# Both feed-forward blocks in two phases, with gated activations stored to DRAM and seven-product sums formed in PSUM

## The chip, the cores and the metric

The kernel runs on one core of a Trainium2 chip. The metric is device time in microseconds for one execution. TensorE (PE) does the matmuls, VectorE (DVE), ScalarE (ACT) and GpSimd (POOL) the elementwise work, SyncE (SP) issues the DMAs. The time before is the median of three runs.

## What is computed

The program is a two-layer encoder trunk over 1024 tokens of width 1024, in float32: in each layer an attention block and a SwiGLU feed-forward block (FFN), both with a modulated RMS norm ahead and a gated residual add behind, and a last RMS norm.

```python
D_FF = 2816
def swiglu(h, w_in, w_out):
    gate, up = jnp.split(h @ w_in, 2, axis=-1)
    return (jax.nn.silu(gate) * up) @ w_out

for i in range(DEPTH):                       # DEPTH = 2
    ...
    h = rmsnorm(x, norm2_g[i]) * (1.0 + scale2) + shift2
    x = x + gate2 * swiglu(h, f_w_in[i], f_w_out[i])
return rmsnorm(x, final_g)
```

## The kernel before

A float32 operand is split into a high part (ACT cast, L95) and a low part (VectorE subtract, L96), and a product is three matmuls: high by high, high by low, low by high (`mm3`, L98 to L107). Activations lie transposed, 128 features by 512 tokens; the tokens are two halves, c = 0 and 1. Weights come in raw blocks of 256 KB (five slots, `RAW`), are combined on POOL where a combination is wanted (L833), and split into one of four pairs of tiles (`RP`).

The FFN (`ffn`, L843) has 22 steps f, one for 128 gate and 128 up features. For f = 2 to 20 the first matmul (1024 by 256 of weights, by 1024 by 1024) is done by `fast(f)`: seven products of half-size blocks in place of eight. Each is 4 x 3 = 12 matmuls of 512 columns, and its operands are combinations of blocks: those of the activations are made once by `norm_parts` (L754) at the start of the FFN, those of the weights by `w_operands` for each f. f = 0, 1 and 21 are done by `plain(f, c)`, four block products for each half of the tokens. The seven products of `fast` rotate over seven half-banks of PSUM (`prod`: two tiles S of two banks each, two T, one A). The sums of products are formed by VectorE adds in SBUF (L902, L918) with a few ACT copies (L926, L928, L941), then Silu and the product gate by up.

After each two f, `out(p)` does the second matmul for their 256 features: four w_out blocks, 96 matmuls, into banks T, T, M in turn (`ffn_out`, L1033), each result added to the residual by VectorE (L1036, `gate2 * ps + x`). These matmuls are placed by priority between the products of the next f. The program's order on each engine is set by a scheduler at build time, from the order of the code and from priority offsets (`WAHEAD`: weight work 60 places earlier). A PSUM tile is waited for as a whole: a user of a tile that is written again waits for the last reader of the tile.

In layer 0 the modulation of layer 1 is computed within the FFN: `ada_half` gives small steps, two per f, each with a raw load, an ACT activation (L147) and a POOL add (L149). In layer 1 the last `out` is split by token half, c = 1 in two quarters; after each the norm's squares are summed (L176, L180), the row sum is formed on PE (L184), VectorE and POOL form the factor (L198, L200), and `final` (L1018) scales and stores.

Of the kernel before, what the change touches and what calls it, by code (L numbers as in the profile page):

```python
# [30 lines left out]
DAHEAD = 0  # L31
MAHEAD = 60
# [6 lines left out]
TAILP = 0, 4  # L39
# [19 lines left out]
class Trunk:  # L59
# [38 lines left out]
    def mm3(self, ps, w, xs, n, w0=0, first=True, last=True):  # L98

        whi, wlo = w  # L100
        mm = self.nc.tensor.matmul
        for k in range(n):
            ws = slice((w0 + k) * P, (w0 + k + 1) * P)
            xh, xl = xs[k]
            mm(ps, lhsT=whi[:, ws], rhs=xh, start=first and k == 0, stop=False)  # L105
            mm(ps, lhsT=whi[:, ws], rhs=xl, start=False, stop=False)  # L106
            mm(ps, lhsT=wlo[:, ws], rhs=xh, start=False, stop=last and k == n - 1)  # L107
# [65 lines left out]
    def norm_acc(self, pool, x, d, box, eng=None, n=CH):  # L173
        nc = self.nc
        sq = self.t(pool, "ft", [P, CH])
        nc.scalar.activation(out=sq[:, :n], in_=x, func=AF.Square)  # L176
        if d == 0:
            box["sq"] = sq
        else:
            (eng or nc.gpsimd).tensor_tensor(out=box["sq"][:, :n], in0=box["sq"][:, :n], in1=sq[:, :n], op=ALU.add)  # L180
# [11 lines left out]
    def norm_rb(self, sq, n=4, ps=None):  # L192
        nc = self.nc
        if ps is None:
            ps = self.bank("A")
        self.rowsum(ps, sq, n)
        v = self.t(self.sp, "v8", [P, 4])
        self.v_ins = nc.vector.tensor_scalar(out=v[:, :n], in0=ps[:, :n], scalar1=1.0 / D, scalar2=EPS, op0=ALU.mult, op1=ALU.add)  # L198
# [552 lines left out]
    def norm_parts(self, ft, bslot, tmp, xs, rb, av, bv, c, h0, ops):  # L751

        nc = self.nc
        h1 = {}  # L754
# [12 lines left out]
        def comb(i, a, b, op, eng=None, eng2=None):  # L767
            t = self.t(ft, "ft", [P, CH])
            (eng or nc.vector).tensor_tensor(out=t, in0=a, in1=b, op=op)
            return lambda: put(i, t, eng2)  # L770

        def step0(d):
            h0[d] = h_of(d, bslot(F32))
            if d < 4:
                put(2, h0[d])
            else:
                comb(4, h0[d], h0[d - 4], ALU.subtract)()

        def step1(d):
            e, f = h_of(d, self.t(ft, "ft", [P, CH])), h_of(d + 4, tmp())  # L780
            comb(3, e, f, ALU.subtract)()
            put(5, f)
            comb(6, h0[d], e, ALU.add, nc.gpsimd, nc.gpsimd)()
            h1[d] = f

        def step2(d):
            f = h1[d]
            p1 = comb(1, h0[d], f, ALU.add, nc.gpsimd)
            p7 = comb(7, h0[d + 4], f, ALU.add)
            p1()  # L790
            p7()
# [14 lines left out]
    def w_split(self, src):  # L806
        hi, lo = self.w_pair()
        raw = self.w_tile(src)
        with self.tc.high_priority(offset=WAHEAD):
            self.split(hi, lo, raw)  # L810
        return hi, lo

    def w_operands(self, layer, f):

        raw = {}

        def blk(i, j):
            if (i, j) not in raw:
# [3 lines left out]

        comb = {1: (1, 1, 2, 2, ALU.add, False), 2: (2, 1, 2, 2, ALU.add, True), 5: (1, 1, 1, 2, ALU.add, False),
                6: (2, 1, 1, 1, ALU.subtract, False), 7: (1, 2, 2, 2, ALU.subtract, True)}

        def get(i):
            hi, lo = self.w_pair()
            if i in comb:
                a, b, c, d, op, last = comb[i]
                x, y = blk(a, b), blk(c, d)  # L830
                t = x if last else y if i == 6 else self.t(self.rw, "raw", [P, CH])
                with self.tc.high_priority(offset=WAHEAD):
                    self.nc.gpsimd.tensor_tensor(out=t, in0=x, in1=y, op=op)  # L833
                    self.split(hi, lo, t)
            else:
                x = blk(*{3: (1, 1), 4: (2, 2), 8: (1, 2), 9: (2, 1)}[i])
                with self.tc.high_priority(offset=WAHEAD):
                    self.split(hi, lo, x)
# [4 lines left out]
    def ffn(self, layer, wo, xdst):  # L843
# [3 lines left out]
        with tc.tile_pool(name="hb", bufs=22, reuse_waits="tile") as hb, \  # L847
# [33 lines left out]
            gs = [[], []]  # L881
            unit = {}
            tt = nc.vector.tensor_tensor
            f_tile = lambda: self.t(ft, "ft", [P, CH])

            flip = [0]

            def prod(i, get):

                n = flip[0] % 7  # L890
                flip[0] += 1
                if n < 4:
                    if n % 2 == 0:
                        unit["S"] = self.t(self.pss, "S")
                    ps = unit["S"][:, n % 2 * CH:(n % 2 + 1) * CH]
                else:
                    ps = self.bank("TTA"[n - 4])
                self.mm3(ps, get(i), ops[i], 4)
                return ps

            def add(t, ps):
                tt(out=t, in0=t, in1=ps, op=ALU.add)  # L902

            def plain(f, c):
# [3 lines left out]
                for h, (i, j) in enumerate((((5, 2), (8, 4)), ((2, 2), (4, 4))) if c == 0 else (((5, 5), (3, 3)), ((9, 3), (2, 5)))):  # L908
# [3 lines left out]
                g = f_tile()  # L912
                nc.scalar.activation(out=g, in_=ps[:, :CH], func=AF.Silu)
                glu(c, g, ps[:, CH:])

            def glu(c, x, y):
                hi, lo = self.t(gp, "g", [P, CH], F32R), self.t(gp, "g", [P, CH], F32R)
                tt(out=x, in0=x, in1=y, op=ALU.mult)  # L918
                self.split(hi, lo, x)
                gs[c].append((hi, lo))  # L920

            def fast(f, mid):

                get = self.w_operands(layer, f)
                gate1, up1, gate0, up0 = (f_tile() for _ in range(4))
                nc.scalar.copy(out=gate1, in_=prod(3, get))  # L926
                p = prod(1, get)
                nc.scalar.copy(out=gate0, in_=p)  # L928
                tt(out=up1, in0=gate1, in1=p, op=ALU.add)
                mid()  # L930
                p = prod(5, get)
                tt(out=gate0, in0=gate0, in1=p, op=ALU.subtract)
                add(gate1, p)
                nc.scalar.activation(out=gate1, in_=gate1, func=AF.Silu)
                add(up1, prod(6, get))
                if ada:
                    ada.pop(0)()
                add(gate0, prod(7, get))
                p = prod(2, get)
                tt(out=up1, in0=up1, in1=p, op=ALU.subtract)  # L940
                nc.scalar.copy(out=up0, in_=p)  # L941
                p = prod(4, get)
                add(gate0, p)
                add(up0, p)
                if ada:
                    ada.pop(0)()
                nc.scalar.activation(out=gate0, in_=gate0, func=AF.Silu)
                glu(1, gate1, up1)
                glu(0, gate0, up0)

            def w_out(p, h):
                return self.w_split(a["w_out"][layer, p, h])

            def out(p):
                cur = [gs[0][:], gs[1][:]]
                gs[0].clear(), gs[1].clear()

                def go():
                    for h in range(4):
                        w = w_out(p, h)  # L960
                        for d in (2 * h, 2 * h + 1):
                            for c in range(2):
                                self.ffn_out(w, cur[c], d, gate2, xs[c][d])

                return go

            for c in range(2):
                for f in range(LEAD):
                    plain(f, c)
# [7 lines left out]
            for c in range(2):  # L977
                plain(NF - 1, c)
            if layer == 0:
                self.make_a(self.avec[1][0], self.sm[:, C_N1 + 8:C_N1 + 16], self.mods[1][1])  # L980
            hn = [[None] * KT, [None] * KT]
            todo = [lambda: None] * KT if layer == 0 else []
            ws = [w_out(NF // 2 - 1, h) for h in range(4)]
            parts = [(0, 0, CH), (1, 0, CH)] if layer == 0 else [(0, 0, CH), (1, 0, CH // 2), (1, CH // 2, CH)]
            for part, (c, n0, n1) in enumerate(parts):
                box = {}
                n = n1 - n0
                xc = [x[:, n0:n1] for x in xs[c]]
                gc = [(hi[:, n0:n1], lo[:, n0:n1]) for hi, lo in gs[c]]
                cs = slice(c * CH + n0, c * CH + n1)  # L990
                if layer:
                    ps = self.t(self.pss, "S") if part else self.bank("A")
                for d in range(KT):
                    self.ffn_out(ws[d // 2], gc, d, gate2, xc[d], n)
                    if layer == 0:
# [207 lines left out]
```

## Time and profile before

| | |
|---|---|
| median of 3 runs | 2751.7 us (2749.83 to 2757.51) |
| the profiled execution | 2753.28 us, span 2751.2 us |
| granted TensorE clock, mean | 0.970 |
| PE busy | 2600.1 us, 95% |
| DVE, ACT, POOL busy | 70%, 43%, 36% |
| DMA, mean | 71 GB/s |

The span runs from the first to the last instruction of the profiled execution. Busy shares are means over the whole program; the FFN of layer 0 fills about 840 to 1480 us of it, that of layer 1 about 2070 to 2740 us. A matmul's shown length (0.39 us for 512 columns) is not its price, since matmuls are pipelined: the distance between two starts is.

### The profile page before, as it was taken

To read this page: it belongs to the slowest core of one execution; us is meant where nothing else is said; L and a number is where in the kernel's file an instruction comes from. 1 tells how busy PE (TensorE), PEld (TensorE's weight loads), DVE (VectorE), ACT (ScalarE), POOL (GpSimd) and SP (SyncE) were. 2 spreads that over 40 slices of the span, in tenths; PEclk is the share of its full clock that TensorE was granted. 3 is DMA by queue.
4 is the path that set the end of the run, shared out by engine and by line. 5 is a ranking of instruction groups with operands and counts; after the bars stand their busy time and mean duration, and the time that the engine had idled before them with its cause. 6 is when DMAs were issued, how large, how long until landed. Compare 5 with 4: busy or idle time off the path is not lost.

```text
span 2751.2 us, 34376 instructions
## 1 busy us (share of the span) xinstructions
PE 2600.1 (95%) x12888; PEld 2138.1 (78%) x12888; DVE 1913.9 (70%) x2921; ACT 1193.2 (43%) x2049; POOL 988.7 (36%) x664
## 2 busy tenths in 40 slices
PE   6799999999998999999999899999998999999997
PEld 5577777777776888888887788888877888888886
DVE  6777777777667667676666777577567666666666
ACT  5455555555443333333334565555443333332323
POOL 7634444531154223232223456433153222222222
PEclk9899999999998999999999999999999999999998
DMA  6211211112211222221214222213211111111112
GB/s 255 74 44 49 70 50 59 63 42 96 78 49 58 66 65 74 65 69 62 71 64 146 96 73 89 85 59 110 70 35 50 54 50 58 54 50 54 50 58 85
DMA packets 86582, 195.89 MB, mean 71 GB/s; under 512 B 9488, under 2 KB 11792, under 8 KB 86416
## 3 DMA queue, kind: packets, MB, share of 16 engines
q1 hardware_dynamic: 86416, 193.71, 20.7%
q8 instruction: 101, 1.65, 0.3%
q14 instruction: 65, 0.53, 0.1%
HBM read 177.94 MB, written 15.73 MB: 70 GB/s over the span
## 4 chain that ended last, share of the span: by engine, by line
PE 76%; DVE 12%; ACT 3%; POOL 3%; DMA 2%; issue 2%; SPq 0%; DVEq 0%; ACTq 0%; POOLq 0%
PE T L105 7%; PE T L106 7%; PE T L107 7%; PE S L106 6%; PE S L105 6%; PE S L107 6%; PE M L105 6%; PE M L106 5%; PE M L107 5%; PE S L548 3%; PE T L256 3%; PE A L270 2%; PE A L268 2%; PE A L269 2%; DVE mx L556 2%
## 5 line engine op out<-in xcount | busy, mean ns | idle before, releaser
L833 POOL TENSOR_TENSOR raw<-raw,raw 128x512 f32<-128x512 f32 x214 | 299.2, 1399 | 877.5 <-DMA raw<-in_w_in 552.1
L95 ACT CAST whi<-raw 128x512 fp32r<-128x512 f32 x402 | 249.0, 621 | 672.1 <-PE T L106 215.7
L96 DVE TENSOR_TENSOR wlo<-raw,whi 128x512 fp32r<-128x512 f32 x402 | 330.3, 826 | 124.8 <-ACT whi L95 124.4
L105 PE MATMUL M<-h,whi 128*128 128x512 f32 x616 | 252.6, 410 | 8.6 <-ACT tmp L470 4.2
L1036 DVE SCALAR_TENSOR_TENSOR h<-T,mod,h 128x512 f32<-128x512 f32 (+1 forms) x270 | 197.7, 733 | 70.8 <-PE T L107 69.6
L107 PE MATMUL M<-h,wlo 128*128 128x512 f32 x616 | 244.6, 397 | 1.0 <-POOL wlo L96 1.0
L105 PE MATMUL S<-h,whi 128*128 128x512 f32 x572 | 226.7, 397 | 19.5 <-DVE ft L918 19.3
L106 PE MATMUL M<-h,whi 128*128 128x512 f32 x616 | 244.9, 398 | 0.0
L95 ACT CAST pt<-T 128x512 fp32r<-128x512 f32 x256 | 145.3, 588 | 211.5 <-PE T L256 211.0
L106 PE MATMUL S<-h,whi 128*128 128x512 f32 x572 | 227.5, 398 | 5.0 <-DVE h L214 3.1
L96 DVE TENSOR_TENSOR pt<-T,pt 128x512 fp32r<-128x512 f32 x256 | 171.6, 682 | 80.7 <-ACT pt L95 80.4
L107 PE MATMUL S<-h,wlo 128*128 128x512 f32 x572 | 226.2, 396 | 0.0
L105 PE MATMUL T<-g,whi 128*128 128x512 f32 (+1 forms) x540 | 210.7, 390 | 10.2 <-DVE h L1036 8.8
L106 PE MATMUL T<-g,whi 128*128 128x512 f32 (+1 forms) x540 | 208.3, 386 | 1.4 <-DVE g L96 1.4
L107 PE MATMUL T<-g,wlo 128*128 128x512 f32 (+1 forms) x540 | 207.9, 385 | 0.0
L129 POOL TENSOR_TENSOR wraw<-wraw,cond 128x1024 f32<-128x1024 f32 x64 | 155.9, 2437 | 126.9 <-DMA wraw<-in_ada_t 119.6
L556 DVE TENSOR_REDUCE mx<-S 128x1 f32<-128x1024 f32 x128 | 150.2, 1215 | 44.3 <-PE S L548 44.2
L270 PE MATMUL A<-pt,v 128*128 128x256 f32 x512 | 155.6, 304 | 23.2 <-DVE pt L96 23.2
L559 ACT ACTIVATE e<-S,mx 128x1024 f32<-128x1024 f32 x128 | 141.4, 1111 | 71.7 <-DVE mx L558 71.7
L256 PE MATMUL T<-ident,e 128*128 128x128 f32 x1024 | 149.1, 280 | 13.3 <-DVE pt L96 10.1
L268 PE MATMUL A<-pt,v 128*128 128x256 f32 x512 | 156.3, 305 | 4.3 <-ACT pt L95 4.2
L269 PE MATMUL A<-pt,v 128*128 128x256 f32 x512 | 151.4, 296 | 0.0
(290 smaller groups left out, 6445.7 us busy)
## 6 DMA issues: line engine op xcount, KB each, us to landing
raw<-in_w_in SPq DMA_DIRECT2D x200, 256.0 KB, 2.8
wraw<-in_ada_t SPq DMA_DIRECT2D x64, 512.0 KB, 3.2
raw<-in_w_out SPq DMA_DIRECT2D x88, 256.0 KB, 2.6
wraw<-in_wqkvA SPq DMA_DIRECT2D x23, 512.0 KB, 3.2
aq<-in_ada_s SPq DMA_DIRECT2D x16, 512.0 KB, 4.9
raw<-in_ada_w SPq DMA_DIRECT2D x32, 256.0 KB, 2.6
wraw<-in_wqkvB SPq DMA_DIRECT2D x15, 512.0 KB, 3.3
o<-tmp SPq DMA_DIRECT2D x28, 256.0 KB, 2.0
```

The lines of the kernel that those rows point to most:

```text
L95: self.nc.scalar.copy(out=hi, in_=src)
L96: (eng or self.nc.vector).tensor_tensor(out=lo, in0=src, in1=hi.bitcast(F32), op=ALU.subtract)
L105: mm(ps, lhsT=whi[:, ws], rhs=xh, start=first and k == 0, stop=False)
L106: mm(ps, lhsT=whi[:, ws], rhs=xl, start=False, stop=False)
L107: mm(ps, lhsT=wlo[:, ws], rhs=xh, start=False, stop=last and k == n - 1)
L256: nc.tensor.transpose(ps[:, i * P:(i + 1) * P], w[:, k * P:(k + 1) * P], self.ident)
L268: mm(ps, lhsT=vh[:, ks], rhs=hi, start=(k == 0), stop=False)
L269: mm(ps, lhsT=vl[:, ks], rhs=hi, start=False, stop=False)
L270: mm(ps, lhsT=vh[:, ks], rhs=lo, start=False, stop=(k == KT - 1))
L556: nc.vector.tensor_reduce(out=mx, in_=ps, op=ALU.max, axis=AX.X, negate=True)
L833: self.nc.gpsimd.tensor_tensor(out=t, in0=x, in1=y, op=op)
L1036: self.nc.vector.scalar_tensor_tensor(out=x, in0=ps, scalar=gate2[:, d:d + 1], in1=x, op0=ALU.mult, op1=ALU.add)
```

## The change

The FFN is done in two phases. Phase 1 computes all gated activations: `fast` for f = 2 to 21 with another scheme of seven products, in which four of the sums are formed in PSUM (`more=True` goes on adding to a bank that holds a former product). One tile S holds x and z, a bank T holds y. ACT copies a state of x or z to SBUF before the next product is added to it. Four POOL combinations of weights per f remain of five. The gated activations and their combinations are stored to DRAM (`keep`, seven kinds for each of eleven pairs of f, 154 stores of 256 KB in all).

Phase 2 computes the second matmul as seven block products over all of k: for each of eleven k a left operand (w_out blocks, `left`), a right one (loaded from DRAM, `right`) and 4 x 3 matmuls into four banks; x stands in banks T, T, A, M, y in the two tiles S. The residual add comes after a product (`add`, L1035). Layer 1's last product goes in two halves of 256 columns. The norm of c = 0 and its finals are issued during product 5. `norm_parts` makes other combinations, four subtractions fewer ahead of the first product. Over the program this is 9108 in place of 9480 matmuls of 512 columns and 1800 in place of 1632 of 256; 198 in place of 88 w_out loads; 154 loads of the stored tiles. The diff, cut to its core:

```diff
-    def mm3(self, ps, w, xs, n, w0=0, first=True, last=True):
+    def mm3(self, ps, w, xs, n, w0=0, first=True, last=True, more=False):
...
-            mm(ps, lhsT=whi[:, ws], rhs=xh, start=first and k == 0, stop=False)
+            mm(ps, lhsT=whi[:, ws], rhs=xh, start=first and k == 0 and not more, stop=False, skip_group_check=more)
...
+            gd = self.tc.dram_tile([7, NP, P, CH], F32, name=f"gd{layer}")
...
+            def prod(ps, i, w):
+                self.mm3(ps, w, ops[i], 4, first=i in (1, 2, 7), more=i in (3, 4, 5, 6))
...
-            def fast(f, mid):
+            def fast(f):
                 get = self.w_operands(layer, f)
+                xz, y = self.t(self.pss, "S"), self.bank("T")
+                x, z = xz[:, :CH], xz[:, CH:]
                 gate1, up1, gate0, up0 = (f_tile() for _ in range(4))
...
+                prod(x, 1, get(1))
+                nc.scalar.copy(out=gate0, in_=x)
+                prod(z, 7, get(7))
+                nc.scalar.copy(out=up1, in_=z)
+                prod(x, 6, get(6))
+                nc.scalar.copy(out=up0, in_=x)
+                prod(y, 2, get(2))
+                tt(out=gate0, in0=gate0, in1=y, op=ALU.add)
+                nc.scalar.activation(out=gate0, in_=gate0, func=AF.Silu)
                 if ada:
                     ada.pop(0)()
+                prod(x, 5, get(5))
+                tt(out=up1, in0=up1, in1=x, op=ALU.add)
+                prod(z, 4, get(4))
+                tt(out=up0, in0=up0, in1=z, op=ALU.add)
                 if ada:
                     ada.pop(0)()
+                prod(x, 3, get(3))
+                nc.scalar.activation(out=gate1, in_=x, func=AF.Silu)
+                a, b = glu(f, 0, gate0, up0), glu(f, 1, gate1, up1)
+                a()
+                b()
...
-            pend = out(0)
-            for f in range(LEAD, NF - 1):
-                fast(f, pend or (lambda: None))
-                pend = out(f // 2) if f % 2 else None
-            for c in range(2):
-                plain(NF - 1, c)
+            for f in range(LEAD, NF):
+                fast(f)
...
+            def right(i, k):
+                t = self.hslot(F32)
+                nc.sync.dma_start(out=t, in_=gd[i - 1, k])
+                hl = self.hpair()
+                with self.tc.high_priority(offset=WAHEAD):
+                    self.split(*hl, t)
+                return hl
...
+            def product(i, ps):
+                for k in range(NP):
+                    w, x = left(i, k, lambda k: self.w_pair()), right(i, k)
+                    for n in range(4):
+                        term(ps[n], w, x, n * P, k, i in (3, 4, 5, 6))
+                    if side and k % 2:
+                        side.pop(0)()
...
+            x = [self.bank(b) for b in "TTAM"]
+            product(1, x)
+            add(x, 0, 0)
+            y = y_banks()
+            product(2, y)
+            add(y, 0, 0, True)
+            product(6, x)
+            add(x, 0, 4)
+            y = y_banks()
+            product(7, y)
+            add(y, 1, 4)
+            product(4, y)
+            add(y, 0, 4, True)
+            side += norm(0, self.t(self.pss, "S")[:, :CH])
+            product(5, x)
+            add(x, 1, 4, True)
```

In `left`, product 2 loads three w_out blocks per k and keeps a sum of two (s1), product 6 loads one and keeps it (s2), product 7 loads two, products 1, 3 and 4 one, and product 5 none.

The order of the built program moves as follows. In a row, an output `S_10068` is tile S number 10068; `h` and `hb` are parts of the activation operands, `whi` and `wlo` of the weights; brackets name the engines that the instruction waits for.

On PE, before, in the FFN of layer 0: the end of one product on tile S_9212, two matmuls of the next product on a bank T, then the second product on S_9170. The first product on S_9170 ended just ahead of the twelve matmuls on S_9212.

```order
L105 MATMUL S_9212<-hb_7483,whi_9213 128x512
L106 MATMUL S_9212<-hb_7484,whi_9213 128x512
L107 MATMUL S_9212<-hb_7483,wlo_9214 128x512
L105 MATMUL T_9260<-hb_7667,whi_9261 128x512 [waits Activation_49]
L106 MATMUL T_9260<-hb_7668,whi_9261 128x512
L105 MATMUL S_9170<-hb_7663,whi_9190 128x512 [waits Activation_49]
L106 MATMUL S_9170<-hb_7664,whi_9190 128x512
L107 MATMUL S_9170<-hb_7663,wlo_9191 128x512
```

The two products that share a tile stood apart by a product on another tile.

On PE, with the change, at a like place of layer 0: the end of product 7 (onto z, second half of S_10068) and the start of product 6 (onto x, the first half).

```order
L106 MATMUL S_10068<-hb_7468,whi_10093 128x512
L107 MATMUL S_10068<-hb_7469,whi_10093 128x512
L108 MATMUL S_10068<-hb_7468,wlo_10094 128x512
L106 MATMUL S_10068<-hb_7639,whi_10114 128x512 [waits Activation_49]
L107 MATMUL S_10068<-hb_7640,whi_10114 128x512
L108 MATMUL S_10068<-hb_7639,wlo_10115 128x512
```

Ten rows on, the end of product 6, two matmuls of product 1 of the next f (S_10223), and product 5 onto x.

```order
L106 MATMUL S_10068<-h_7669,whi_10114 128x512
L107 MATMUL S_10068<-h_7670,whi_10114 128x512
L108 MATMUL S_10068<-h_7669,wlo_10115 128x512
L106 MATMUL S_10223<-h_7197,whi_10229 128x512 [waits Activation_49]
L107 MATMUL S_10223<-h_7198,whi_10229 128x512
L106 MATMUL S_10068<-h_7408,whi_10160 128x512 [waits Activation_49]
L107 MATMUL S_10068<-h_7409,whi_10160 128x512
L108 MATMUL S_10068<-h_7408,wlo_10161 128x512 [waits DVE_49]
```

Products 7 and 6 now follow each other in the same tile. Product 6's first matmul waits for ACT up to L943. In the same way the next f's product 2 starts with two matmuls between products 4 and 3, behind a wait for ACT.

On ACT, with the change, the rows that these waits are for: the cast of product 3's weights (`whi_10198`), L943 the copy of z, the cast of the next product 1's weights (`whi_10229`), L945 the copy of x.

```order
L948 ACTIVATE ft_10072<-ft_10072 128x512 [waits DVE_49]
L96 CAST whi_10198<-raw_10137 128x512 [waits PE_49,Pool_49]
L943 COPY ft_10071<-S_10068 128x512 [waits PE_49]
L96 CAST whi_10229<-raw_10231 128x512 [waits DMAHW5_49,PE_49]
L945 COPY ft_10073<-S_10068 128x512 [waits PE_49]
```

Each copy now stands behind a cast. The cast of `whi_10198` waits for the last matmul but one of product 7, whose high part lay in that tile, and the cast of `whi_10229` for the last but one of product 6. The order repeats for every f from 2 on, in both layers; in layer 0 two modulation steps (L148) stand between later casts.

## Rows read from the trace of the kernel before

**Rows 1.** The page: the span, and the line of busy times.

```profile
span 2751.2 us, 34376 instructions
...
PE 2600.1 (95%) x12888; PEld 2138.1 (78%) x12888; DVE 1913.9 (70%) x2921; ACT 1193.2 (43%) x2049; POOL 988.7 (36%) x664
```

**Rows 2.** The page: the chain that ended last, by engine.

```profile
PE 76%; DVE 12%; ACT 3%; POOL 3%; DMA 2%; issue 2%; SPq 0%; DVEq 0%; ACTq 0%; POOLq 0%
```

**Rows 3.** Windows: us, busy (count) of PE, PEld, DVE, ACT, POOL; PEclk, DMA share, GB/s.

```profile
2100.00:2707.00 607.00, 601.37 (x2638) 493.97 (x2637) 398.92 (x571) 186.03 (x315) 134.14 (x98) 1.00 0.16 53
855.00:1476.00 621.00, 615.36 (x2715) 505.92 (x2714) 412.08 (x581) 208.90 (x352) 172.82 (x126) 1.00 0.21 67
1484.00:1496.00 12.00, 11.70 (x56) 9.48 (x55) 8.60 (x11) 7.75 (x12) 8.13 (x6) 1.00 1.02 388
```

**Rows 4.** Waits of PE, 2100 to 2707 us: total us, times, longest us.

```profile
PE T L105 <- DVE h L1036: 4.2, 7, 0.6
PE T L106 <- DVE g L96: 0.7, 2, 0.5
PE T L105 <- ACT ft L941: 0.6, 1, 0.6
```

**Rows 5.** Timeline of PE at 2718 us: start, length, instruction.

```profile
2718.18 0.39 PE L107 MATMUL T<-g,wlo 128*128 128x512 f32 x1
2718.40 0.28 PE L105 MATMUL M<-g,whi 128*128 128x256 f32 x1
2718.52 0.28 PE L106 MATMUL M<-g,whi 128*128 128x256 f32 x1
```

**Rows 6.** Timeline of PE at two waits, 2160 and 2228 us.

```profile
2160.68 0.39 PE L107 MATMUL M<-g,wlo 128*128 128x512 f32 x1
2161.63 0.50 PE L105 MATMUL T<-g,whi 128*128 128x512 f32 x1 [0.56 <-ACT ft L941]
2161.97 0.39 PE L106 MATMUL T<-g,whi 128*128 128x512 f32 x1
...
2227.98 0.39 PE L107 MATMUL M<-g,wlo 128*128 128x512 f32 x1
2228.96 0.50 PE L105 MATMUL T<-g,whi 128*128 128x512 f32 x1 [0.60 <-DVE h L1036]
```

**Rows 7.** Waits of PE, 2064 to 2080 us.

```profile
PE S L105 <- DVE ft L918: 9.7, 1, 9.7
```

**Rows 8.** Window of 8 us at the start of layer 1's FFN, columns as in 3.

```profile
2068.00:2076.00 8.00, 4.63 (x10) 3.14 (x10) 8.00 (x8) 5.09 (x10) 7.37 (x6) 0.50 0.18 63
```

**Rows 9.** Timeline of DVE at 2051 us.

```profile
2051.00 0.68 DVE L96 TENSOR_TENSOR wlo<-raw,whi 128x512 fp32r<-128x512 f32 x1
2051.60 1.79 DVE L96 TENSOR_TENSOR h<-g,h 128x512 fp32r<-128x512 f32 x1
```

**Rows 10.** Timeline of the tail: PE, SP's queue, PE.

```profile
2732.44 0.28 PE L107 MATMUL T<-g,wlo 128*128 128x256 f32 x1
...
2739.08 0.33 SPq L1031 DMA_DIRECT2D out_t<-hb  x1
...
2740.45 1.02 PE L184 MATMUL S<-ones,ft 128*128 128x1 f32 x4 [7.73 <-DVE ft L180]
```

**Rows 11.** Timeline of ACT at 2160 us, and of PE and ACT at 2699 us.

```profile
2160.99 0.58 ACT L941 COPY ft<-T 128x512 f32<-128x512 f32 x1 [0.81 <-DVE ft L940]
...
2698.91 0.39 PE L106 MATMUL S<-hb,whi 128*128 128x512 f32 x1
...
2699.38 0.62 ACT L95 CAST whi<-raw 128x512 fp32r<-128x512 f32 x1
```

**Rows 12.** Groups by line, 855 to 1476 us: the modulation's ACT and POOL steps.

```profile
L149 POOL TENSOR_TENSOR acc<-acc,raw 128x512 f32<-128x512 f32 x28 | 36.6, 1308 | 87.0 <-ACT raw L147 87.0
...
L147 ACT ACTIVATE raw<-raw,cond 128x512 f32<-128x512 f32 x28 | 20.3, 724 | 65.9 <-DMA raw<-in_ada_w 65.9
```

**Rows 13.** The page, DMA issues: KB each, us to landing.

```profile
raw<-in_w_in SPq DMA_DIRECT2D x200, 256.0 KB, 2.8
```

More of the change, by code (lines that the diff above doesn't have):

```diff
@@ L981, in ffn @@
+            box = [{}, {}]
             hn = [[None] * KT, [None] * KT]
[L982 to L995, printed above, removed]
[L996 to L1012 removed]
@@ L1013, in ffn, with load, left @@
[L1013 to L1018 removed]
+            side = []
+            def load(pool, tag, blk, k):
+                t = self.t(pool, tag, [P, CH])
+                nc.sync.dma_start(out=t, in_=w_out[blk, k])
+                return t
+            def left(i, k, pair):
+                hi, lo = pair(k)
+                raw = lambda blk: load(rw, "raw", blk, k)
+                sub = lambda o, x, y: tt(out=o, in0=x, in1=y, op=ALU.subtract)
+                if i == 2:
+                    s1.append(load(hb, "hb", 2, k))
+                    u = raw(3)
+                elif i == 6:
+                    s2.append(load(hb, "hb", 0, k))
+                elif i == 7:
+                    u = raw(0)
+                t = s2[k] if i == 6 else s1[k] if i == 5 else raw({1: 0, 2: 1, 3: 1, 4: 3, 7: 2}[i])
+                with self.tc.high_priority(offset=WAHEAD):
+                    if i == 3:
+                        sub(t, t, s2[k])
+                    elif i == 6:
+                        sub(t, s1[k], t)
+                    elif i == 7:
+                        sub(t, t, u)
+                    self.split(hi, lo, t)
+                    if i == 2:
+                        tt(out=s1[k], in0=s1[k], in1=u, op=ALU.add)
+                return hi, lo
@@ new lines, in right, with term @@
+            def right(i, k):
+                t = self.hslot(F32)
+                nc.sync.dma_start(out=t, in_=gd[i - 1, k])
+                hl = self.hpair()
+                with self.tc.high_priority(offset=WAHEAD):
+                    self.split(*hl, t)
+                return hl
+            def term(ps, w, x, o, k, more):
+                self.mm3(ps, [t[:, o:o + P] for t in w], [x], 1, first=k == 0 and not more, last=k == NP - 1, more=more)
+            def product(i, ps):
[5 more added lines that the diff above has]
+                        side.pop(0)()
@@ new lines, in add @@
+            def add(ps, c, d0, done=False, n0=0, n1=CH):
+                for n in range(4):
+                    d = d0 + n
+                    x = xs[c][d][:, n0:n1]
+                    with self.tc.high_priority(offset=EAHEAD):
+                        nc.vector.scalar_tensor_tensor(out=x, in0=ps[n][:, n0:n1], scalar=gate2[:, d:d + 1], in1=x, op0=ALU.mult, op1=ALU.add)
+                if done:
+                    for d in range(d0, d0 + 4):
+                        if layer == 0:
+                            nc.sync.dma_start(out=xdst[d, :, c * CH:(c + 1) * CH], in_=xs[c][d])
+                        self.norm_acc(ft, xs[c][d], box[c], nc.vector if c and d0 == 0 else None)
@@ new lines, in ffn @@
+            product(1, x)
[13 more added lines that the diff above has]
+            add(x, 1, 4, True)
+            if layer == 0:
+                product(3, x)
+                add(x, 1, 0, True)
+                for s in side + norm(1, None):
+                    s()
+                return hn
```

252 lines of the change are left out of this document (115 added, 137 removed).

## The prediction

> **What bounds the kernel now.** I read the page first. TensorE is busy for 95% of the span [rows 1] and makes 76% of the chain that ended last [rows 2], so the time is the number of matmuls times their pitch, plus the gaps. Then I read the two FFN windows: 601.37 us of 607 and 615.36 of 621 busy, clock 1.00 [rows 3]. In the list of waits the 607 us hold ten waits, 5.5 us together, and the other layer's list reads the same [rows 4]. They also give the price of a matmul, 601.37 over 2638: 0.228; in the timeline the starts lie 0.22 to 0.23 us apart for 512 columns and 0.12 for 256 [rows 5]; I use 0.227. So the old FFN runs within 2% of its matmuls. Such a kernel gains by fewer matmuls or by less at its ends, and loses by each wait that is put between two products. The order decides whether new waits have cover.
>
> **The parts that gain.** Matmuls: 9480 to 9108 of 512 columns, 372 x 0.227 = -84.3; 1632 to 1800 of 256, 168 x 0.12 = +20.2; together **-64**. Old stalls: at each, 0.98 us lie between two starts in place of 0.227 (2227.98 to 2228.96), and the next start follows after 0.34 [rows 6], so 0.87 are lost; ten per layer, twenty in all: **-17**. They came from the second matmul's adds (L1036) in banks T, T, M, and that interleaved matmul is gone.
>
> Start of each FFN: PE waits 9.7 us for L918 [rows 7], on a VectorE that is busy without a break (8.00 of 8.00 us, PE's clock 0.50 [rows 8]). Its operations take from 0.68 to 1.79 us [rows 9], eight in the 8.00 us. The new operand steps leave three fewer ahead of the first product; at about 0.9 each that is -2.7 per layer, **-5** (0 to -11).
>
> Tail: the last matmul with weights starts at 2732.44; the row sum of the last quarter starts only at 2740.45, after VectorE's backlog of finals and adds, and the span ends at 2751.2 [rows 1, 10], 18.8 us after the matmul. In the new order the finals of the first half lie in product 5, so the 8.0 us ahead of the row sum shrink to a last add, square and add with their hand-overs, some 2 us: **-6** (0 to -8). The 10.7 us from the row sum on stay.
>
> **The waits that the change adds.** In the order ahead of this text, product 6 (onto x) follows 7 (onto z) with nothing between and waits for ACT. x and z are halves of one PSUM tile, and the value that 6 waits for is reached by L943, the copy of z, though 6 doesn't touch z. And this copy stands on ACT behind the cast of product 3's weights, which waits until 7 has released its pair (only four pairs). The prices come from rows: ACT starts 0.47 us after the start of the releasing matmul (2698.91 to 2699.38), a cast takes 0.62, a copy 0.58 to 0.59 [rows 11]; PE starts 0.06 after ACT ends (2161.57 to 2161.63 [rows 6, 11]), and its next start comes 0.34 later in place of 0.227, 0.11 more [rows 6]. Per f:
> - 7 to 6: the pair is released by the last matmul but one. So 0.24 after the last one's start the cast begins, 0.86 it ends, the copy of z ends at 1.45, PE starts at 1.51: 1.51 - 0.227 + 0.11 = **1.39**. If the copy went first it would be 0.47 + 0.59 + 0.06 - 0.227 + 0.11 = 1.00.
> - after 6: the next f's product 1 needs the pair that 6 has just released: 0.24 + 0.62 + 0.06 - 0.227 + 0.11 = **0.80**. Its two matmuls then just cover the copy that product 5 waits for.
> - after 4: the next product 2 likewise, **0.80**. The add on z (L954) that product 3 waits for lies behind it.
>
> Product 4's wait (add on x) has ten matmuls of cover, 2.3 us; it costs nothing, and 0.47 + 0.68 + 0.06 - 0.227 + 0.11 = 1.1 if they were gone [rows 9, 11]. The sum is 2.99 per f; with the copy first 2.60; if ACT also starts a little earlier (the copy at 2160.99 starts 0.31 after a matmul's start at 2160.68 [rows 6, 11], but waited for VectorE), 2.4. I take 2.8, since the order shows the cast ahead: 40 f x 2.8 = **+112** (96 to 124).
>
> The rule against which I weighed the 0.11: the Trainium skill, TensorE: Matmul & The Clock Gate, Architectural detail, says that PE's queue can pull weight loads ahead of matmuls in flight, by which a matmul after a wait would find its weights loaded. The trace speaks against it: 0.34 between the first two starts after a wait [rows 6]. By the page the sum would be 13 us smaller.
>
> Layer 0 has two more links in 18 of its 20 f: the modulation steps (ACT 0.72, POOL 1.31 [rows 12]) each wait for a load of 2.8 us [rows 13] into one of five raw slots and stand on ACT ahead of casts and of the copy that product 7 waits for. Two loads, two ACT and two POOL steps are 9.7 us, and the next copy is due some 11 us after product 5; so it is nearly hidden, and a late load shows. Cost 0 to 2 us per f: 0 to 36, taken as **+10**.
>
> **Phase 2.** Its operands go out and come back: 154 stores, 154 loads and 110 more w_out loads of 256 KB. A product of 11 k is 132 matmuls, 30 us. SyncE issues in 0.33 us each [rows 10], 176 loads per layer, 58 of the seven products' 209 us. 176 x 262 KB in 209 us are 221 GB/s, in product 2 alone, with four tiles a k, 1.05 MB in 2.72 us, 386 GB/s; the trace shows 388 GB/s with the queues full [rows 3]. Up to eleven k of the second operand can be there ahead, as product 1 needs half as much. VectorE has at most three operations per k, 2.1 of 2.72 us. No PSUM wait is worse than one per product. So I charge one fill per change of product: **+3** for both layers, 0 to 20 in all. That cover, prefetch over several k, is what rival C takes away.
>
> **Sum** against the profiled execution's 2753.3: -64 - 17 - 5 - 6 + 112 + 10 + 3 = +33, 2786.3. The median of the three runs, 2751.7, is 1.6 lower, so I say **2785**. The measurement tells about 0.3% (8 us) from no change: 2743 to 2760 counts as the same.
>
> **Rivals.**
> A, the matmul saving wins. If 6 did not have to wait for z, 7 to 6 would cost nothing, and were the casts timely too, all would be gain: 2753.3 - 92 + 3 = 2664; with the two cast waits alone left at 0.72 it is 40 x 1.44 = 58 more, about 2722, with layer 0's 10 about 2732. For it: the old order also keeps two products in one tile, and its trace shows ten short waits in 607 us [rows 4]. Against: there the twelve matmuls of another tile stand between a tile's two products, here none. Chance 0.10 (2664 to 2740).
> The Trainium skill, PSUM — Partial Sum Buffer, Terms, forbids two engines only in the same bank and same partitions, and x and z are separate banks, so the chip itself would let 6 start; by that rule A's 2722 holds. The order shows a wait all the same.
>
> B, no change: the short price, 2.4 per f (+96), nothing extra in layer 0 and in phase 2: 2753.3 - 92 + 96 = 2757. It decides if ACT starts 0.31 and not 0.47 after a release. Chance 0.12.
>
> C, phase 2 is limited by supply. Product 2 needs all of the 388 GB/s. If a quarter less comes, 290, a k takes 3.6 us there and not 2.7: 0.9 x 11 = 10 per layer, 20 in both, from the point at which the prefetched operands are used up; product 7 (three tiles a k, 289 GB/s) is then just served, and loses as much if the two tiles per k that it passes through five raw slots take 7 us each from issue to release. So 2805 to 2825. Against it: the other products need two tiles a k or one, and a load now takes 2.8 [rows 13]. Chance 0.10.
>
> D, the clock falls. It is 0.50 at the FFN start, where PE had waited 9.7 us [rows 7, 8], and 1.00 where its waits are 0.6 at most [rows 3, 4]; no row shows gaps of 1.4. If it stood at 0.50 in a tenth of the 40 f (some 87 us at 0.50, 43 us lost), about 2828. Chance 0.02.
>
> **How the numbers follow.** Forecast 0.66, from 2755 (the copy first, 104, and nothing in layer 0 or phase 2: 21 less, and a start and tail 9 better) to 2830 (124, 36 and 20 would be 55 more; not all three come together). Faster by over 0.3% is A, 0.10; the same is B, 0.12; slower is the rest, 0.78. The range 2748 to 2835 leaves out A and the ends of C and of the forecast.
>
> **What would show it.** In the new profile's first phases the period of one f should be some 21.8 us in place of 84 x 0.227 = 19.0. The list of waits should name three releasers about forty times each: ACT ft L943 for S at product 6 (about 1.1 us idle), ACT whi L96 twice (0.5 us idle each); busy share about 88%, clock 1.00. Phase 2 should be dense at a pitch of 0.227 with DMA near 220 GB/s, the tail about 12 us. I am wrong in the main term if L943 is no releaser; wrong in phase 2 if DMA releases PE there for more than 5 us per layer; A is right if the period of an f is below 20 us.

## The result, and the profile after

The changed kernel takes 2823.4 us (median of four runs, 2819.8 to 2830.3), the kernel before 2753.4 beside it: a ratio of 1.0257, 95% interval 1.0231 to 1.0282. It is 70 us slower. The forecast was 2785 with a range of 2748 to 2835: the sign was right and the time lies in the range, but of the loss only 33 us were forecast.

The page of the changed kernel, its span, its line of busy times and the chain by engine:

```profile
span 2820.5 us, 35123 instructions
...
PE 2570.1 (91%) x12684; PEld 2076.0 (74%) x12684; DVE 1783.6 (63%) x2736; ACT 1255.5 (45%) x2175; POOL 923.1 (33%) x614
...
PE 19%; DVE 2%; ACT 2%; issue 2%; DMA 1%; DVEq 0%; POOLq 0%; SPq 0%; POOL 0%; ACTq 0%
```

PE is busy for 30 us less than before [rows 1], and the span is 69 us longer: about 100 us of idle time of PE have come in. The chain's shares add up to 26% here, where PE alone had 76% in [rows 2], so the chain tells little; I use the waits. They are, over the whole span (total us, times, longest us):

```profile
PE S L106 <- ACT ft L943: 53.3, 40, 3.5
PE S L106 <- DVE g L919: 24.7, 2, 12.4
...
PE S L106 <- ACT whi L96: 21.3, 39, 3.0
PE T L106 <- ACT whi L96: 20.6, 41, 1.0
```

Beside ten short waits per FFN [rows 4] stand now 120 waits of 95 us, and they are the three per step that the order showed. Their period is read from the copy of z, which comes once per f, 20 times in each layer (first and last start; layer 0 above, layer 1 below):

```profile
L943 ACT COPY ft<-S x20: 577/578/580, 863.3 to 1293.6; 128x512 f32<-128x512 f32 x20
...
L943 ACT COPY ft<-S x20: 577/578/579, 2146.1 to 2569.7; 128x512 f32<-128x512 f32 x20
```

(1293.6 - 863.3) / 19 = 22.65 us per f in layer 0, (2569.7 - 2146.1) / 19 = 22.29 in layer 1, where 84 matmuls at 0.227 are 19.04. The losses are 3.61 and 3.25 per f, 137 us over the 40.

One period in layer 1, PE's timeline, each wait with the matmul ahead of it (start, length, instruction, idle time and what ended it):

```profile
2300.32 0.39 PE L108 MATMUL S<-hb,wlo 128*128 128x512 f32 x1
2301.73 0.50 PE L106 MATMUL S<-hb,whi 128*128 128x512 f32 x1 [1.02 <-ACT ft L943]
...
2304.36 0.39 PE L108 MATMUL S<-h,wlo 128*128 128x512 f32 x1
2305.23 0.50 PE L106 MATMUL S<-h,whi 128*128 128x512 f32 x1 [0.48 <-ACT whi L96]
...
2313.32 0.39 PE L108 MATMUL S<-hb,wlo 128*128 128x512 f32 x1
2314.19 0.50 PE L106 MATMUL T<-h,whi 128*128 128x512 f32 x1 [0.48 <-ACT whi L96]
...
2322.26 0.39 PE L108 MATMUL S<-hb,wlo 128*128 128x512 f32 x1
2324.15 0.50 PE L106 MATMUL S<-hb,whi 128*128 128x512 f32 x1 [1.51 <-ACT ft L943]
```

The last matmul of a product and the first of the next lie 1.41 or 1.89 us apart at product 6, 0.87 at the two others, in place of 0.227. At the two casts the loss is 0.48 + 0.27: the 0.27 are the 0.16 by which a matmul's shown length exceeds its pitch (0.39 against 0.227), and 0.11 at the restart. ACT at the two places of product 6:

```profile
2300.57 0.62 ACT L96 CAST whi<-raw 128x512 fp32r<-128x512 f32 x1 [1.10 <-PE S L107]
2301.09 0.58 ACT L943 COPY ft<-S 128x512 f32<-128x512 f32 x1
...
2322.48 0.63 ACT L948 ACTIVATE ft<-ft 128x512 f32<-128x512 f32 x1 [2.12 <-DVE ft L947]
2323.01 0.60 ACT L96 CAST whi<-raw 128x512 fp32r<-128x512 f32 x1
2323.52 0.58 ACT L943 COPY ft<-S 128x512 f32<-128x512 f32 x1
```

At 2300.57 the cast stands ahead of the copy of z, as forecast. At 2322.48 a Silu stands ahead of both, and the wait is 0.5 us longer. It comes late since VectorE was late with the sum it works on:

```profile
2320.07 1.78 DVE L908 TENSOR_TENSOR g<-g,g 128x512 f32<-128x512 f32 x1
2321.77 0.68 DVE L947 TENSOR_TENSOR ft<-ft,T 128x512 f32<-128x512 f32 x1
```

L908 makes a combination of gated activations; such combinations follow every second f. It takes 1.78 us, and L947, which makes gate0 ready for the Silu, stands behind it.

In phase 2 PE is dense in some places and not in others. Two windows that lie mostly in product 2, in layer 0 and layer 1 (columns as in [rows 3]):

```profile
1330.00:1360.00 30.00, 30.00 (x134) 24.86 (x133) 27.20 (x44) 10.63 (x20) 0.00 (x0) 1.00 0.81 266
...
2610.00:2640.00 30.00, 30.00 (x133) 24.69 (x132) 26.91 (x44) 10.81 (x19) 0.00 (x0) 1.00 0.85 269
```

Product 2, the heaviest on loads, loses nothing here: its 132 matmuls into the S tiles take 29.9 us from 1336.5 and 30.0 us from 2613.6. Two windows further on:

```profile
1450.00:1480.00 30.00, 24.87 (x100) 19.72 (x99) 16.49 (x25) 10.35 (x18) 6.97 (x5) 0.83 0.34 123
2640.00:2670.00 30.00, 27.35 (x110) 21.23 (x109) 20.23 (x29) 14.24 (x26) 4.18 (x3) 0.94 0.45 145
```

At 0.227 a window holds 132 matmuls; here 100 (with 16 small ones of the norm) and 110, at a granted clock of 0.83 and 0.94. Both lie at a change of product, behind products 4 and 2. The DMAs of the page (KB each, us to landing):

```profile
raw<-in_w_in SPq DMA_DIRECT2D x192, 256.0 KB, 2.7
...
h<-gd SPq DMA_DIRECT2D x154, 256.0 KB, 3.9
raw<-in_w_out SPq DMA_DIRECT2D x154, 256.0 KB, 3.2
...
hb<-in_w_out SPq DMA_DIRECT2D x44, 256.0 KB, 4.4
```

A stored tile lands after 3.9 us, where a load of the same size took 2.8 before [rows 13] and w_in still takes 2.7. The w_out blocks that phase 2 keeps (`hb`), which were never stored by the kernel, take 4.4, so the longer time is not shown to come from the detour through DRAM.

The tail is as forecast. Its last matmul and the last row sum, by PE's timeline:

```profile
2809.17 0.28 PE L108 MATMUL M<-h,hb 128*128 128x256 f32 x1
2811.07 0.58 PE L187 MATMUL S<-ones,ft 128*128 128x1 f32 x4 [1.63 <-DVE ft L183]
```

The row sum follows the last matmul after 1.9 us (8.0 before [rows 10]), and the span ends 11.3 us behind the matmul, 7.5 less than before.

### The profile page after: what moved, and what is told of

It reads as the page before. It is cut to its first block, busy times and chain, and to the rows that moved or that the text cites. A ratio compares the mean times of both kernels' runs of the same rounds, so it can differ in the third digit from the quotient of the medians.

```text
span 2820.5 us, 35123 instructions
## 1 busy us (share of the span) xinstructions
PE 2570.1 (91%) x12684; PEld 2076.0 (74%) x12684; DVE 1783.6 (63%) x2736; ACT 1255.5 (45%) x2175; POOL 923.1 (33%) x614
## 5 line engine op out<-in xcount | busy, mean ns | idle before, releaser
L97 DVE TENSOR_TENSOR wlo<-raw,whi 128x512 fp32r<-128x512 f32 x415 | 325.4, 786 | 335.9 <-ACT whi L96 331.3
L96 ACT CAST whi<-raw 128x512 fp32r<-128x512 f32 x415 | 256.1, 619 | 525.1 <-PE S L107 450.2
L106 PE MATMUL S<-h,whi 128*128 128x512 f32 x968 | 387.1, 400 | 49.4 <-DVE g L919 24.7
L107 PE MATMUL S<-h,whi 128*128 128x512 f32 x968 | 381.4, 394 | 4.5 <-DVE h L217 4.5
L108 PE MATMUL S<-h,wlo 128*128 128x512 f32 x968 | 380.8, 393 | 0.5 <-DVE wlo L97 0.5
L106 PE MATMUL M<-h,whi 128*128 128x512 f32 (+1 forms) x701 | 285.3, 407 | 9.6 <-ACT tmp L473 5.9
L108 PE MATMUL M<-h,wlo 128*128 128x512 f32 (+1 forms) x701 | 276.7, 395 | 1.0 <-POOL wlo L97 1.0
L107 PE MATMUL M<-h,whi 128*128 128x512 f32 (+1 forms) x701 | 277.5, 396 | 0.0
L106 PEld LDWEIGHTS S<-h,whi 128*128 128x128 f32 x968 | 183.9, 190 | 113.0 <-ACT whi L96 39.0
L96 ACT CAST pt<-T 128x512 fp32r<-128x512 f32 x256 | 145.6, 589 | 192.8 <-PE T L259 191.6
L97 DVE TENSOR_TENSOR pt<-T,pt 128x512 fp32r<-128x512 f32 x256 | 172.0, 684 | 83.2 <-ACT pt L96 82.8
L106 PE MATMUL S<-hb,whi 128*128 128x512 f32 x432 | 173.7, 402 | 53.3 <-ACT ft L943 53.3
L107 PEld LDWEIGHTS S<-h,whi 128*128 128x128 f32 x968 | 184.1, 190 | 40.7 <-DVE h L217 4.9
L108 PEld LDWEIGHTS S<-h,wlo 128*128 128x128 f32 x968 | 184.0, 190 | 40.6 <-DVE wlo L97 1.2
L96 ACT CAST h<-h 128x512 fp32r<-128x512 f32 x166 | 102.1, 618 | 184.4 <-DMA h<-gd 183.4
L97 DVE TENSOR_TENSOR h<-h,h 128x512 fp32r<-128x512 f32 x166 | 126.3, 765 | 91.0 <-ACT h L96 90.7
L273 PE MATMUL A<-pt,v 128*128 128x256 f32 x512 | 153.5, 300 | 22.7 <-DVE pt L97 22.7
```

Source lines behind the costliest of these rows:

```text
L96: self.nc.scalar.copy(out=hi, in_=src)
L97: (eng or self.nc.vector).tensor_tensor(out=lo, in0=src, in1=hi.bitcast(F32), op=ALU.subtract)
L106: mm(ps, lhsT=whi[:, ws], rhs=xh, start=first and k == 0 and not more, stop=False, skip_group_check=more)
L107: mm(ps, lhsT=whi[:, ws], rhs=xl, start=False, stop=False, skip_group_check=more)
L273: mm(ps, lhsT=vh[:, ks], rhs=lo, start=False, stop=(k == KT - 1))
```

## The experiments

Two theories stood for phase 1. W: a PSUM tile is waited for as a whole, so the shared tile makes the waits. S: the supply of weights sets the period. Two for phase 2. B: the residual adds, squares and POOL adds at the end of a product come in a burst, ahead of the operand splits. D: the operands land late.

**z in a tile of its own** (2720.6 us, ratio to before 0.9874, 0.9860 to 0.9889)

```diff
-                x, z = xz[:, :CH], xz[:, CH:]
+                x, z = xz[:, :CH], self.bank("A")
```

> Edit: z gets a tile of its own (bank A), x stays in the first half of S; nothing else. Theory W (waits on a whole tile): product 6 no longer waits for the copy of z. The trace of the changed kernel lists 53.3 us in 40 waits on that copy, and each wait loses 0.27 us more than is listed (0.16 of the pipelined last matmul, 0.11 at the restart), so 64 us go; the two waits per step on weight casts stay. Time about 2760 (2745 to 2775), period of a step f about 20.7 in place of 22.3 to 22.7. Rival S (supply): weight loads and POOL's combinations set the period, and the wait only moves to another releaser: 2813 to 2830.

It gained 103 us, ends 24 us below theory W's range, and is faster than the kernel before. Two rows of PE's waits, then the copy of z in layers 0 and 1:

```profile
PE T L107 <- DVE h L97: 11.9, 11, 2.6
...
PE S L106 <- ACT whi L96: 5.4, 3, 4.4
...
L943 ACT COPY ft<-A x20: 579/597/602, 862.8 to 1229.5; 128x512 f32<-128x512 f32 x20
...
L943 ACT COPY ft<-A x20: 579/597/599, 2093.8 to 2456.5; 128x512 f32<-128x512 f32 x20
```

The copy of z is no releaser any more; the period is (1229.5 - 862.8) / 19 = 19.30 us in layer 0 and 19.09 in layer 1, close to the matmuls' own 19.04.

The waits on casts are gone as well, 5.4 us in three, with the same four pairs. In the order built for this kernel product 4 stands between product 6 and the next f's product 1, so the pair that 6 releases is cast under twelve matmuls. With the shared tile product 1 followed 6 directly. So the waits on casts were no want of pairs. The order moved at the other wait too: between 7 and 6 stand now the former f's product 3 and product 2, 24 matmuls or 5.4 us in nearly every f, and in 39 of the 40 the copy of z is done before 6 starts, so that a wait for it would cost nothing. In the one step left, in layer 0, the copy (A) and the start of 6 (S) overlap:

```profile
960.88 0.59 ACT L943 COPY ft<-A 128x512 f32<-128x512 f32 x1
...
961.15 0.41 PE L106 MATMUL S<-hb,whi 128*128 128x512 f32 x1
```

So 6 doesn't wait for z any more, as W has it. In the other 39 steps, and at the casts, the order that the scheduler now builds is by itself enough for the gain; the bank and the order, which came with one line, were not tried apart. The Trainium skill, PSUM — Partial Sum Buffer, Terms, bars two engines from the same bank and the same partitions at a time. These two rows agree: PE starts into x's bank 0.32 us before ACT has done with z's.

S falls. Over 19 periods in each layer 125 us went, and 103 in all: some 20 came back behind the last step, where PE now waits for splits of h (first row). Phase 2 starts earlier there and loads the same; that it finds fewer operands loaded ahead is argued, not tried.

**Five pairs** (2836.9 us, ratio 1.0292, 1.0275 to 1.0309) and its control, **six ft tiles alone** (2830.9 us, ratio 1.0269, 1.0250 to 1.0288)

```diff
-RP = 4
+RP = 5
-FT = 8
+FT = 6
...
-                gate1, up1, gate0, up0 = (f_tile() for _ in range(4))
+                gate0, up1, up0, gate1 = (f_tile() for _ in range(4))
```

> Edit: five pairs of split weight tiles in place of four; for the space six ft tiles in place of eight, allocated in the order of their first use. x and z still share a tile. Theory W: with a pair to spare, a cast no longer waits for the product that has just ended, so the 80 listed waits on casts (41.9 us, 0.27 more each: 63 us) go for the most part, and the copy of z no longer stands behind a cast (0.5 of each of 40 waits, 20 us): about 2745 (2730 to 2785). Rival S: 2813 to 2830. If the waits on casts stay while the pairs are there, another thing (the raw blocks or POOL) gives the casts late.

The control has the edit but for the first two lines.

> Control for the run with five pairs: four pairs as in the changed kernel, but six ft tiles in place of eight. If the six tiles are what took the gain of the fifth pair (theory F), this is slower than the five-pair run's 2836.9: 2850 to 2900, the difference being what the fifth pair gives. If the six tiles are harmless, 2816 to 2830, and the fifth pair itself made it slower by some 14, by the other order that it led to.

Both missed: five pairs were to gain some 80 us, and the control lies in neither of its ranges. The six tiles cost 8 us by the medians, though the two intervals overlap, and the fifth pair gained nothing on top. With it the waits read:

```profile
PE S L106 <- ACT ft L941: 60.3, 38, 3.1
...
PE S L106 <- ACT whi L96: 25.2, 40, 5.0
...
PE T L106 <- ACT whi L96: 18.8, 38, 0.8
```

With a pair more, the casts still release PE 78 times, and product 7 now waits for L941, the copy of x, which it doesn't touch, as product 6 waited for the copy of z. The wait on the shared tile changed its place. My reading of the two waits on casts as a lack of pairs was wrong.

**Both edits** (2777.8 us, ratio 1.0088, 1.0066 to 1.0110)

> Edit: both edits together, z in bank A and five pairs with six ft tiles. Theory W: all three waits per step go, 64 + 63 = 127 us: about 2696 (2680 to 2730), faster than the kernel before by some 2%. Period of a step f about 19.1 to 19.5, 84 matmuls at 0.227. Rival S: 2800 or more, since supply stays; in between (2730 to 2770), one of the two edits' gain is taken by a new wait.

A miss: 57 us slower than the own tile alone. The two rows that are new in PE's waits:

```profile
PE S L106 <- ACT ft L958: 24.1, 32, 0.8
...
PE S L108 <- DVE wlo L97: 16.2, 27, 1.1
```

PE now waits for L958, the Silu behind product 3, ahead of product 1, and low parts of weights come late. Six ft tiles hold the gate and up tiles of one f and a half; that this is what makes L958 a wait was not tried.

**The norm of the first half spread over the next products** (2813.2 us, ratio 1.0212, 1.0196 to 1.0228)

```diff
-                        self.norm_acc(ft, xs[c][d], box[c], nc.vector if c and d0 == 0 else None)
+                        acc = lambda d=d: self.norm_acc(ft, xs[c][d], box[c], nc.vector if c and d0 == 0 else None)
+                        acc() if c else side.append(acc)
...
-            side += norm(0, self.t(self.pss, "S")[:, :CH])
+            side.append(lambda: side.extend(norm(0, self.t(self.pss, "S")[:, :CH])))
```

> Edit, in phase 2 alone: the squares and adds of the norm of the first token half are issued one per two k within the next product, and the row sum after them, in place of all at once at the end of products 2 and 4. Theory B (burst): the stalls seen after products 2 and 4 (5 us in layer 1 near 2655, 10 in layer 0 near 1470, with the clock at half afterwards) come from residual adds, squares and POOL's adds that stand ahead of operand splits on VectorE and ACT and ahead of the row sum on PE; spread out they cost 10 to 20 us less: 2803 to 2813. Rival D (supply by DMA): the splits are late since their tiles land late (3.9 us to landing in place of 2.7): no change, 2817 to 2830.

10 us went. The same two windows:

```profile
1450.00:1480.00 30.00, 30.00 (x134) 24.84 (x133) 21.68 (x30) 15.22 (x27) 7.29 (x4) 1.00 0.51 167
2640.00:2670.00 30.00, 28.91 (x126) 23.31 (x125) 21.73 (x31) 16.53 (x30) 4.92 (x3) 1.00 0.42 141
```

134 and 126 matmuls in place of 100 and 110, the clock at 1.00. In layer 0 this is the gain: from its last copy of z to the first one of layer 1 (L943) the traces give 844.2 us in place of 852.5. In layer 1 nothing is left of it: from the last copy to the end 251.6 us in place of 250.8, since the last row sum now waits longer, 4.9 us in place of 1.6:

```profile
PE S L187 <- DVE ft L183: 4.9, 1, 4.9
```

B holds for the stalls at both places, and as time for layer 0.

**Half of the stored tiles loaded** (2807.9 us, ratio 1.0189, 1.0174 to 1.0204)

```diff
-                t = self.hslot(F32)
-                nc.sync.dma_start(out=t, in_=gd[i - 1, k])
+                if k % 2 == 0:
+                    kept[0] = self.hslot(F32)
+                    nc.sync.dma_start(out=kept[0], in_=gd[i - 1, k])
+                t = kept[0]
```

> The changed kernel, with the stored operand of phase 2 loaded for every other k only; the k between is split from the same loaded tile again (a part of the second matmul's operand is left out so). Matmuls, splits and adds stay; 70 of 154 loads go. Theory D (tiles land late): the waits on h in phase 2 go: 2803 to 2813. Theory B (the burst of adds and squares) and a late split by VectorE's and ACT's own queues: 2817 to 2830.

15 us went, as D forecast. The same windows:

```profile
1450.00:1480.00 30.00, 24.87 (x106) 19.72 (x105) 17.47 (x27) 10.48 (x18) 6.97 (x5) 0.87 0.31 105
2640.00:2670.00 30.00, 29.01 (x128) 23.71 (x127) 22.84 (x32) 13.37 (x25) 4.14 (x3) 1.00 0.33 106
```

The second place, behind product 2, is dense (128), as with the spread norm (126): there the burst and the late tiles act together, and either edit fills the window. The first place, behind product 4, keeps its stall (106), which the spread norm alone took away. From layer 0's last copy of z to layer 1's first the trace gives 838.3 us in place of 852.5, 14 of the 15; from layer 1's last copy to the end only 1 us went. The sign that D had named, no more waits on h, is seen in part: PE's waits for splits of h (L96, L97) go from 3.0 us to none in layer 1 (2590 to 2800 us), and only from 6.1 to 5.5 in layer 0 (1300 to 1525). So the loads cost time; through which wait in layer 0 stays open.

**Own tile and spread norm together** (2710.6 us, ratio 0.9828, 0.9812 to 0.9844)

> Edit: z in bank A and the spread norm of the first token half, the two edits that gained alone (2720.6 and 2813.2). Theories W and B act in different phases, so the gains add: 2720.6 less 8 to 12 is 2710 (2703 to 2717). If the operand supply sets the stalls of phase 2 (theory D), phase 2 now starts with less loaded ahead, and the spread norm gains nothing more: 2717 to 2725.

The gains add by the medians: 10 us again. The profiled execution (2717.8 us) is the longest of its four and 1.6 us under that of the own tile alone, so the trace doesn't show where they lie.

**The stored tiles' loads on GpSimd's queue** (2809.5 us, ratio 1.0200, 1.0175 to 1.0225), else as the last

```diff
-                nc.sync.dma_start(out=t, in_=gd[i - 1, k])
+                nc.gpsimd.dma_start(out=t, in_=gd[i - 1, k])
```

> As the run with z in bank A and the spread norm, and the loads of the stored operand issued by GpSimd's queue in place of SyncE's. Theory Q: on SyncE's queue these loads stand behind w_out loads that wait for a raw slot (some 100 us of such waits per layer in the trace), so they are issued late; on a queue of their own they are ahead, and phase 2 loses 8 to 20 us less than with the same kernel on SyncE: 2690 to 2702. If the rate or the landing time is what counts, no change against it: 2703 to 2717.

A miss of the other sign: 99 us slower than the last. PE's longest row of waits, a row of the DMA queues, and a load on POOL's timeline:

```profile
PE T L107 <- DVE h L97: 37.4, 17, 5.8
...
q0 software_dynamic: 12320, 40.38, 4.3%
...
1272.45 0.54 POOL L1012 DMA_DIRECT2D h<-gd  x1 [12.00 <-PE M L108]
```

PE waits for splits of h. The load waits for PE: for a slot that a matmul has yet to release, 12.0 us in this case. That the loads were issued only when a slot came free, and not far ahead, is the likely cause, not a tried one: the page lists this queue as another kind (software_dynamic; SyncE's is hardware_dynamic), so the edit changed two things. The time to landing is nearly the same, 4.0 us in place of 3.7.

**The sums of w_out blocks formed in product 6** (2688.6 us, ratio 0.9755, 0.9741 to 0.9769), else as the one with own tile and spread norm

```diff
-                if i == 2:
+                if i == 6:
                     s1.append(load(hb, "hb", 2, k))
                     u = raw(3)
-                elif i == 6:
                     s2.append(load(hb, "hb", 0, k))
...
                     elif i == 6:
+                        tt(out=s1[k], in0=s1[k], in1=u, op=ALU.add)
                         sub(t, s1[k], t)
...
-                    if i == 2:
-                        tt(out=s1[k], in0=s1[k], in1=u, op=ALU.add)
```

> As the run with z in bank A and the spread norm (2710.6), and the sums s1 of two w_out blocks, which products 5 and 6 need, are loaded and formed in product 6 and not in product 2: products 1 and 2 then need two tiles a k, 6 four, 7 three. Theory D (tiles land late in product 2, where DMA moves 356 to 359 GB/s with its engines full): the stalls of product 2 shrink, and by product 6 more is loaded ahead: 2695 to 2705. If the stall only moves to product 6, or VectorE's order there makes it worse: 2707 to 2725.

It gained 22 us, more than forecast. The 30 us from 1260 in layer 0, the start of phase 2, without and with this edit:

```profile
1260.00:1290.00 30.00, 27.87 (x113) 21.91 (x112) 25.63 (x41) 10.35 (x18) 0.00 (x0) 0.94 0.75 243
```

```profile
1260.00:1290.00 30.00, 30.00 (x134) 24.72 (x133) 19.63 (x31) 12.55 (x22) 0.00 (x0) 1.00 0.63 203
```

113 matmuls become 134, and DMA moves 203 GB/s there in place of 243. Product 2, which forms an operand from one block, had loaded two more that only later products use. The next 30 us, again without and with the edit, show that a part of the stall moved on to product 6, as the rival had it. Product 6 takes 36.8 us in layer 0 and 35.9 in layer 1, where it took 32.9 and 34.5:

```profile
1290.00:1320.00 30.00, 26.80 (x107) 19.10 (x107) 19.99 (x27) 12.52 (x23) 4.26 (x3) 1.00 0.68 211
```

```profile
1290.00:1320.00 30.00, 24.80 (x94) 18.72 (x93) 28.54 (x43) 12.51 (x21) 4.22 (x3) 0.89 0.76 254
```

By the traces the seven products of both layers together are 11 us shorter; the rest of the gain lies mostly behind them, on the way to layer 1's FFN, and was not traced. (The 356 to 359 GB/s named in the expectation are from windows of product 1, before product 2.) This is the fastest version of the study, 2.45% under the kernel before. It still pays for the spread norm at the end: 15.0 us from the last matmul with weights to the end of the span, in place of 11.3 in the changed kernel.

## Why the prediction was right in sign and short in size

The parts, in us against the kernel before; forecast, then measured in the two profiled executions (+69 in their spans):

| part | forecast | measured |
|---|---|---|
| matmuls, and the old stalls | -81 | -81 (taken as forecast) |
| start of the FFNs | -5 | about 0 |
| tail | -6 | -7.5 |
| waits of the 40 steps f | +122 | +137 |
| phase 2 and the way on from it | +3 | +24 (what is left, with any error of the first row) |
| outside the FFNs | 0 | -3 |

- The step **"waits that the change adds"** was right in kind: three waits per f with the releasers named, the cast ahead of the copy of z, the clock at 1.00 through the steps, the period 22.3 and not 19.0. It was short by 0.45 per f in layer 1. The three waits by themselves cost 1.29 + 0.75 + 0.75 = 2.79, the 2.8 that I took. The Silu, which in every second f comes late behind VectorE's combinations and stands ahead of the copy, adds 0.5 there, 0.25 per f; the last 0.2 are starts that stand 0.23 to 0.25 apart for some matmuls behind a restart. Layer 0, which alone has the modulation, loses 0.36 more per f, 7 us; 10 were taken.
- The 0.11 at a restart held: the start after 2301.73 comes 0.34 later. The 0.47 from a releasing matmul to ACT's start held too (the cast at 2300.57 starts 0.25 behind the last matmul, 0.24 forecast), but by luck: in the row that it was read from, ACT had no wait and was just ending another cast (2698.72, 0.62 long).
- "Only four pairs" was a wrong cause of a right number, so that number was luck: with the same four pairs and an own tile PE waits for casts no more.
- **"So I charge one fill per change of product: +3"** is the step that failed. It measured +24 in place of +3. It took prefetch as cover and looked at rates. What it missed: the norm of the first half is one chain through ACT, POOL, PE and VectorE that PE meets in the midst of phase 2 (10 us by the spread norm, in layer 0), and the loads of stored tiles cost time (15 us by the run with half of them, 14 of them in layer 0's phase 2 and behind it). Both edits fill the same stall behind product 2 of layer 1, so that their sum comes near the +24 proves nothing about it. The sign that I had set for it, DMA as PE's releaser, could not show: between a load and its matmul stands the split, and it is splits (h L96, h L97), adds and casts that release PE in phase 2.
- Rival C put the loss at product 2. In the changed kernel product 2 is dense, 29.9 and 30.0 us for its 132 matmuls; it loses only when phase 1 is shorter, 36.8 and 37.0 us in the run with z in a tile of its own.
- "Start, -5": PE goes on behind the first gated product 2 us earlier after the norm's factor (30.0 us against 31.9 in layer 1), but it has waited 12.4 us by then and not 9.7. From the norm's factor to the last Silu of the plain steps, windows of both layers give 118.8 us with 388 matmuls before and 112.4 with 360 after: 30.7 us lost in both.
- Rival A asked what happens if 6 need not wait for z; the first experiment comes near that case, by an own tile. It gave 2720.6, where A had 2722 to 2732, but that is luck, by another sum: the casts went too, and phase 2 took some 20 us back.

## What to carry to other kernels

Where two accumulations that alternate share one PSUM tile, look at the built order for a wait on the other half's reader, and give each its own tile if a bank is free: one line was worth 103 us here, together with the order that the scheduler then built. A wait on a weight cast may come from the order and not from the buffer count, so try the order first. When a product's operands make a detour through DRAM, count tiles per k for each product, move loads that only later products need to where there is room, and spread norms over the products that follow them, but look at the end: here the last row sum waited 3.3 us longer for it.

## What was not expected

The granted clock fell after a short wait in phase 2 and stayed up after a longer one. PE's timeline in layer 1:

```profile
2658.49 0.50 PE L107 MATMUL T<-h,whi 128*128 128x512 f32 x1 [1.97 <-DVE h L97]
...
2659.06 0.63 PE L106 MATMUL T<-h,whi 128*128 128x512 f32 x1
2659.48 0.63 PE L107 MATMUL T<-h,whi 128*128 128x512 f32 x1
```

After 1.97 us of waiting, and two starts at the old distance, the starts lie 0.42 to 0.43 apart from 2659.06 to 2662.47, the lower of the clock's two levels (granted 0.53 from 2659.0 to 2662.6), and 0.23 again afterwards. After 2.50 us at 1294.26, with dense work on both sides, the pitch stayed at 0.23. What tells the two cases apart is not shown. And a DMA queue of its own went with a loss: 99 us in the run on GpSimd's queue.
